# Attention scores and value products from high and low parts, one head at a time

## The chip, the core and the metric

The kernel runs on one core of a Trainium2 chip. The time is the device time of that core in microseconds (us). Three runs of the kernel before gave 1809.98, 1813.17 and 1820.33 us, so the median is 1813.17. The profile comes from a fourth execution of 1814.06 us, of which 1812.3 us lie between the first and the last instruction; the granted TensorE clock was 0.999 of full speed in it.

The engines are named as the profile names them: PE is TensorE (matrix products; PEld is its weight load), DVE is VectorE, ACT is ScalarE, POOL is GpSimd, SP is SyncE, which issues most DMAs.

## What is computed

Two layers over 256 latent tokens and 256 context tokens of width 2048. Layer 0 projects both streams, runs 16 heads of neighbourhood attention beside a bidirectional state-space mixer (SSD) of 8 groups, joins their outputs and projects them back. Layer 1 is a gated short convolution between two projections. Each layer's norm is modulated by a vector that is computed from a conditioning input with large weights. What matters here is the attention of one head (the reference, cut):

```
q = rms_norm(heads(p[Q]), q_norm_g);  k = rms_norm(heads(p[K]), k_norm_g);  v = heads(p[V])
s_lat = q @ k_window.T * scale + bias;   s_lat = where(mask, s_lat, -inf)
s_ctx = q @ k_ctx.T * scale
pr = softmax(concat([s_lat, s_ctx]))
out = pr @ concat([v_window, v_ctx]);   out = out * silu(gate_a)
```

Per head that is 256 queries against 512 keys (256 latent, with the window as an added mask, and 256 context) of 128 channels. All inputs are fp32.

## The kernel before

**Products in parts.** The large projections do not use full fp32 products. An operand is split into a high part, rounded to the type fp32r, and a low part, the rest: ACT casts (H = fp32r(w)), DVE subtracts (L = w - H). A product is then three fp32r products, H x H, H x L and L x H, that are summed in PSUM. For the weights this is done chunk by chunk: 1024 columns a chunk, cast by ACT at L409, subtracted by DVE at L416, into three buffers each (`wH`, `wL`). Small products, those of attention and of SSD among them, are done in full fp32 on the unsplit operands.

**Order of the work.** The kernel is written as one Python program that emits every engine's instructions in an order of its own. The main thread emits the projections for PE in a fixed order: in layer 0 the columns of K, V, Q and B of group 0 while the conditioning arrives, then for each of four head groups `a` (four heads each) Q, K, gate, V and the SSD columns, then the output projection `w_out`, then layer 1. Everything else is a task, a generator that yields what it waits for. Between the products, `pump` lets each task run on whose operands a table of costs and due times (`Plan`) counts as ready, so that attention, SSD and norms are woven into the stream of projections. Tasks have three classes: urgent, side (heads and SSD groups) and back. The one back task, `gemv_gen`, multiplies the conditioning weights on DVE (256 multiply-adds at L803, in 16 groups, each closed by four small matrix products into `mrow`) whenever DVE is ahead. The first four groups feed the end of layer 0, the twelfth (n = 11) is needed for the norm of layer 1 (`turn_gen` turns the new stream and scales it), the last before the output.

Each engine works its queue in the emitted order. PE's products wait for the splits of the weights; a wait at the head of ACT's or DVE's queue also holds back the weight splits behind it.

**One head.** `head_gen(a, h)` first loads the head's bias, adds the mask (L1003), and waits for `KT` and `QT`, the group's normed and transposed keys and queries. Then, for each half `qt` of the queries: one full fp32 product of 128 x 128 by 128 x 512 (`score`, L1008), bias and maximum on DVE (L1013), exp on ACT (L1018), scaling on DVE (L1023), four transposes on PE and a copy into `P` on ACT (L1050). `P` has two buffers, `PT0` and `PT1`, taken by even and odd heads. Last, four full fp32 products of 128 x 128 by 128 x 256 add up the values (L1058), DVE multiplies with the gate (L1062), and the head's output goes to the tensor `mixd` in DRAM. A head starts when the head two before it has done its value products. The output projection reads `mixd` back (L1491) and splits it (L1496 on ACT, L1497 on DVE).

Of the kernel before, what the change touches and what calls it, by code (L numbers as in the profile page):

```python
# [8 lines left out]
F32 = mybir.dt.float32  # L9
F32R = mybir.dt.float32r  # L10
AF = mybir.ActivationFunctionType
ALU = mybir.AluOpType
# [129 lines left out]
def kernel(ctx: ExitStack, tc, x, cx, ada_w, ada_b, w_in, w_out, sc_in, sc_out, rpb, small, const,  # L142
# [7 lines left out]
    V, S, G, T, DMA = nc.vector, nc.scalar, nc.gpsimd, nc.tensor, nc.sync  # L150
    DMA2 = nc.scalar
    plan = Plan()
    E = plan.add

    def st(shape, tag, dt=F32, name=None):
        return sb.tile(list(shape), dt, tag=tag, name=name or tag, bufs=1)
# [23 lines left out]
    KT, QT, Vt, gt = st([128, 4, 512], "KT"), st([128, 4, 256], "QT"), st([128, 4, 512], "Vt"), st([128, 4, 256], "gt")  # L180
    sz, xtm, yi = st([128, 4, 256], "sz"), st([128, 2, 512], "xtm"), st([128, 4, 256], "yi")
    PT = [st([128, 4, 256], f"PT{k}") for k in range(2)]
# [12 lines left out]
    four = lambda ap: ap.rearrange("p (a b) -> p a b", a=4)  # L195

    def mm(o, l, r, start, stop):
        E(T.matmul(o, l, r, start=start, stop=stop, skip_group_check=True))  # L198
# [7 lines left out]
    got = set()  # L206
# [128 lines left out]
    def bank():  # L335
        return take(free_b)

    def give(pool, *bs):
        pool.extend(bs)

    W_ = lambda eng, *aps, nb=0: (eng, aps, nb)
    when = lambda f: ("if", f, 0)
# [14 lines left out]
    RAW, HL = {}, {}  # L357
# [178 lines left out]
    for a in range(1, 4):  # L536
        qk = [(w_in, CQ(a), 512), (w_in, CK(a), 512)]
# [226 lines left out]
    bias = [st([128, 3, 256], f"bias{k}") for k in range(2)]  # L764
# [222 lines left out]
        got.add((key, a))  # L987

    b0 = rpbs[0, :, :]
    s4s = [st([128, 8], f"s4_{k}") for k in range(4)]  # L990

    def head_gen(a, h):
        hd = 4 * a + h
        bt, s4, P = bias[hd % 2], s4s[hd % 4], PT[hd % 2]
        yield when(lambda: hd < 2 or ("pv", hd - 2) in got)
        yield W_("SP")
        for r in range(4):
            E(DMA.dma_start(bt[64 * (r % 2):64 * (r % 2) + 64, r // 2, :].rearrange("p (a b) -> p a b", a=4),
                            bass.AP(tensor=b0.tensor, offset=b0.offset + hd * 64 * 320 + (7 - r) * 31 - 61,
                                    ap=[[319, 64], [31, 4], [1, 64]])))  # L1000
        yield W_("DVE", bt)
        bv = bt[:, 0:2, :].rearrange("p q (r c) -> p (q r) c", c=64)
        E(V.tensor_tensor(out=bv, in0=bv, in1=mask.unsqueeze(1).to_broadcast([128, 8, 64]), op=ALU.add))  # L1003
        sps = {}

        def score(qt):
            ps = bank()
            mm(ps, QT[:, h, qt * 128:(qt + 1) * 128], KT[:, h, :], True, True)  # L1008
            return ps

        def top(qt, ps):
            sp = sps[qt] = tmp()
            E(V.tensor_tensor_reduce(out=two(sp), in0=two(ps), in1=bt[:, 1:3, :] if qt else bt[:, 0::2, :], scale=1.0,  # L1013
                                     scalar=-3.0e38, op0=ALU.add, op1=ALU.max, accum_out=s4[:, qt:qt + 1]))
            give(free_b, ps)
            E(V.tensor_scalar(out=s4[:, 2 + qt:3 + qt], in0=s4[:, qt:qt + 1], scalar1=-1.0, scalar2=None, op0=ALU.mult))
            yield W_("ACT", sp, s4)
            E(S.activation(sp, sp, AF.Exp, bias=s4[:, 2 + qt:3 + qt], scale=1.0, accum_out=s4[:, 4 + qt:5 + qt]))  # L1018

        def scale_(qt):  # L1020
            sp = sps[qt]
            E(V.reciprocal(s4[:, 6 + qt:7 + qt], s4[:, 4 + qt:5 + qt]))
            E(V.tensor_scalar(out=sp, in0=sp, scalar1=s4[:, 6 + qt:7 + qt], scalar2=0.5, op0=ALU.mult, op1=ALU.mult))  # L1023

        def trans(qt):
            pt = bank()
            for kt in range(4):
                turn(pt[:, kt * 128:(kt + 1) * 128], sps[qt][:, kt * 128:(kt + 1) * 128])
            give(free_t, sps[qt])
            return pt  # L1030

        yield when(lambda: ("K", a) in got and ("Q", a) in got)
        yield ("grow", 2, 0)
        yield W_("PE", KT[:, h, :], QT[:, h, :], nb=1)
        p0 = score(0)
        yield W_("DVE", p0)
        yield from top(0, p0)
        yield W_("PE", nb=1)
        p1 = score(1)
        yield W_("DVE", p1)  # L1040
        yield from top(1, p1)
        yield W_("DVE", sps[0])
        scale_(0)
        yield W_("DVE", sps[1])
        scale_(1)
        for qt in range(2):
            yield W_("PE", sps[qt], nb=1)
            pt = trans(qt)
            yield W_("ACT", pt)
            E(S.copy(P[:, :, qt * 128:(qt + 1) * 128], four(pt)))  # L1050
            give(free_b, pt)
        yield ("cap", 0, 0)
        yield when(lambda: ("V", a) in got and ("G", a) in got)
        yield ("grow", 0, 1)
        yield W_("PE", P, Vt, nb=1)
        po = bank()
        for kt in range(4):
            mm(po[:, :256], Vt[:, kt, h * 128:(h + 1) * 128], P[:, kt, :], kt == 0, kt == 3)  # L1058
        got.add(("pv", hd))
        yield W_("DVE", po)  # L1060
        o = half()
        E(V.tensor_tensor(out=o, in0=po[:, :256], in1=gt[:, h, :], op=ALU.mult))  # L1062
        give(free_b, po)
        attn[0] += 2
        yield from put_mix(hd, o)
# [450 lines left out]
    def res_gen(k, c0, ps):  # L1516
# [29 lines left out]
    r1 = st([128, 2], "r1")  # L1546
    h1 = {}
    rb1 = []
    late = [PT[0][:, k, :] for k in range(4)] + [PT[1][:, k, :] for k in range(4)] + \
        [xtm[:, k // 2, (k % 2) * 256:(k % 2) * 256 + 256] for k in range(4)] + [yi[:, k, :] for k in range(4)]  # L1550

    held = {}

    def turn_gen():
        yield when(lambda: n_back[0] >= 11.5 and attn[0] == 32 and ssd_done[0] == 8)
        E(V.scalar_tensor_tensor(out=A1, in0=M1[:, 1], scalar=1.0, in1=P_("g1"), op0=ALU.add, op1=ALU.mult))
        for kp in range(0, KB, 2):
            yield when(lambda: ("x1", kp // 4) in got and (kp < 8 or len(passed) == 4))
            yield W_("PE", x1[0][:, kp * 128:(kp + 2) * 128], x1[1][:, kp * 128:(kp + 2) * 128], nb=1)
            pt = bank()  # L1560
            for b in range(2):
                for t in range(2):
                    turn(pt[:, b * 256 + t * 128:b * 256 + (t + 1) * 128], x1[t][:, (kp + b) * 128:(kp + b + 1) * 128])
            for b in range(2):
                kb = kp + b
                if kp < 8:
                    yield W_("ACT", pt)
                    E(S.activation(late[kb], pt[:, b * 256:(b + 1) * 256], AF.Copy, scale=A1[:, kb:kb + 1]))
                else:

                    held[kb] = pt
                got.add(("turn", kb))
            if kp < 8:
                give(free_b, pt)
        keep_up(8)
# [194 lines left out]
    for i in range(4):  # L1770
        for part, gen in ((1, cg_gen), (2, hv_gen), (0, bg_gen), (3, gg_gen)):
            ps = banks(4)
# [23 lines left out]
    for n in range(4):  # L1796
        if n == 1:
            force(lambda: n_back[0] >= 15, (urgent, back))
        ps = banks(2)
# [57 lines left out]
```

## Time and profile before

| | |
|---|---|
| median of 3 runs | 1813.17 us |
| the profiled execution | 1814.06 us |
| its span, first to last instruction | 1812.3 us |
| PE busy | 1775.1 us (98%) |
| DVE busy | 1259.2 us (69%) |
| ACT busy | 775.3 us (43%) |
| score products (L1008) | 32 in 64 records, 259.6 to 1181.5 us |
| value products (L1058) | 64 in 128 records, 277.0 to 1196.3 us |
| layer 1 begins | about 1360 us |

A full fp32 product shows as two matmul records, an fp32r product as one. Matmul records overlap, and the busy time of PE is time in which at least one is open, so what a product costs is read from the distance between starts or ends. Rows of the order of time begin with the start and the length in us; a bracket at the end gives the engine's idle time before the row and what ended it. Rows of groups give busy us, the mean length of one in ns, and the idle time before them. In rows of stretches the columns are named ahead of the rows.

### The profile page before, as it was taken

The page shows a single profiled execution, that of the slowest core. Times are in us where ns is not written, and L with a number is a line of the kernel's source. Part 1 is how long each engine was busy: PE and PEld are TensorE (multiplying, and loading weights), DVE is VectorE, ACT ScalarE, POOL GpSimd, SP SyncE. Part 2 cuts the span into 40 slices and gives each one's busy share as a digit, 9 for nine tenths or more (in the row PEclk, how much of TensorE's full clock was granted, in tenths as well). Part 3 has the DMA queues.
Part 4 walks back from the last instruction along what each step waited for, and adds up shares of the span by engine and source line. Part 5 has one row for each costly group of instructions (what it writes and reads, how often), then busy time and mean ns, then how long its engine had stood idle before and what let it go on. Part 6 is the DMA issues. An engine that isn't in the chain of part 4 may idle for free.

```text
span 1812.3 us, 26337 instructions
## 1 busy us (share of the span) xinstructions
PE 1775.1 (98%) x9961; PEld 1487.4 (82%) x9961; DVE 1259.2 (69%) x2041; ACT 775.3 (43%) x1362; POOL 30.5 (2%) x28
## 2 busy tenths in 40 slices
PE   5999999999999999999999999999999999999998
PEld 4677888888888888888888898778878888888887
DVE  5566875887575887575887687666667866665665
ACT  5422543455232455232454344544435444444442
POOL 0000100000000000000001000000000000000000
PEclk9999999999999999999999999999999999999999
DMA  9987654576655576655576566668776776666564
GB/s 337 342 289 254 196 163 135 169 217 202 204 168 168 170 220 198 218 165 169 170 221 186 165 185 185 205 211 300 268 248 203 241 231 188 190 192 188 192 211 153
DMA packets 249216, 376.90 MB, mean 208 GB/s; under 512 B 32656, under 2 KB 104048, under 8 KB 249088
## 3 DMA queue, kind: packets, MB, share of 16 engines
q1 hardware_dynamic: 239792, 366.64, 63.8%
q10 hardware_dynamic: 9296, 8.57, 1.4%
q8 instruction: 78, 1.28, 0.3%
q14 instruction: 50, 0.41, 0.1%
HBM read 368.70 MB, written 7.77 MB: 208 GB/s over the span
## 4 chain that ended last, share of the span: by engine, by line
PE 92%; DMA 3%; DVE 2%; issue 1%; ACT 1%; SPq 0%; POOL 0%; POOLq 0%; DVEq 0%; ACTq 0%
PE bank L198 90%; PE bank L202 3%; DMA raw<-in_ada_w 2%; DVE wL L416 1%; DVE acc L803 1%; DMA tmp<-dram_mixd 0%; DMA tmp<-dram_csr 0%; DVE hL L752 0%; SPq L566 0%; ACT wH L409 0%; DVE tmp L748 0%; ACT hH L746 0%; DVE xm L612 0%; ACT mix L1496 0%; DVE tmp L1790 0%
## 5 line engine op out<-in xcount | busy, mean ns | idle before, releaser
L409 ACT CAST wH<-raw 128x1024 fp32r<-128x1024 f32 (+1 forms) x440 | 459.0, 1044 | 701.2 <-PE bank L198 576.1
L416 DVE TENSOR_TENSOR wL<-raw,wH 128x1024 fp32r<-128x1024 f32 (+1 forms) x440 | 532.1, 1213 | 257.3 <-ACT wH L409 255.9
L198 PE MATMUL bank<-h,wH 128*128 128x512 f32 x1024 | 357.2, 395 | 2.7 <-ACT h L1636 1.5
L198 PE MATMUL bank<-hH,wH 128*128 128x256 f32 (+1 forms) x1040 | 352.6, 339 | 0.9 <-ACT wH L409 0.9
L198 PE MATMUL bank<-hL,wH 128*128 128x256 f32 (+1 forms) x1040 | 336.9, 324 | 0.0
L198 PE MATMUL bank<-hH,wL 128*128 128x256 f32 (+1 forms) x1024 | 331.2, 323 | 0.5 <-DVE wL L416 0.5
L198 PE MATMUL bank<-h,wL 128*128 128x256 f32 x1024 | 284.5, 278 | 0.0
L198 PE MATMUL bank<-wH,hH 128*128 128x512 f32 x640 | 257.4, 403 | 4.8 <-ACT hH L746 2.6
L198 PE MATMUL bank<-wL,hH 128*128 128x512 f32 x640 | 249.8, 391 | 0.3 <-DVE wL L416 0.3
L198 PE MATMUL bank<-wH,hL 128*128 128x512 f32 x640 | 249.3, 390 | 0.1
L803 DVE SCALAR_TENSOR_TENSOR acc<-raw,csil,acc 128x512 f32<-128x512 f32 x256 | 191.9, 750 | 65.5 <-DMA raw<-in_ada_w 52.0
L198 PEld LDWEIGHTS bank<-h,wH 128*128 128x128 f32 x1024 | 192.1, 188 | 49.1 <-issue 2.2
L198 PEld LDWEIGHTS bank<-hH,wH 128*128 128x128 f32 x1040 | 197.8, 190 | 23.2 <-issue 7.5
L198 PEld LDWEIGHTS bank<-hL,wH 128*128 128x128 f32 x1040 | 197.9, 190 | 19.8 <-issue 5.3
L198 PEld LDWEIGHTS bank<-hH,wL 128*128 128x128 f32 x1024 | 194.6, 190 | 16.5 <-DVE wL L416 1.1
L198 PEld LDWEIGHTS bank<-h,wL 128*128 128x128 f32 x1024 | 192.4, 188 | 0.0
L198 PE MATMUL bank<-wH,mix 128*128 128x512 f32 x512 | 164.1, 397 | 2.2 <-ACT wH L409 2.2
L198 PEld LDWEIGHTS bank<-wH,hH 128*128 128x128 f32 x640 | 120.2, 188 | 35.6 <-issue 7.5
L198 PEld LDWEIGHTS bank<-wH,hL 128*128 128x128 f32 x640 | 120.1, 188 | 25.4 <-DVE hL L752 0.6
L198 PEld LDWEIGHTS bank<-wL,hH 128*128 128x128 f32 x640 | 120.2, 188 | 24.3 <-DVE wL L416 1.1
L198 PEld LDWEIGHTS bank<-wH,mix 128*128 128x128 f32 x512 | 96.9, 189 | 23.4 <-ACT wH L409 2.7
L198 PE MATMUL bank<-wL,mix 128*128 128x512 f32 x256 | 100.6, 393 | 3.8 <-DVE wL L416 3.8
(244 smaller groups left out, 1662.9 us busy)
## 6 DMA issues: line engine op xcount, KB each, us to landing
raw<-in_w_in SPq DMA_DIRECT2D x209, 512.0 KB, 4.5
raw<-in_ada_w SPq DMA_DIRECT2D x163, 512.0 KB, 4.7
raw<-in_sc_in SPq DMA_DIRECT2D x128, 512.0 KB, 3.7
raw<-in_w_out SPq DMA_DIRECT2D x64, 512.0 KB, 4.3
raw<-in_sc_out SPq DMA_DIRECT2D x32, 512.0 KB, 4.5
tmp<-dram_csr SPq DMA_DIRECT2D x32, 256.0 KB, 7.1
PT<-in_ada_w SPq DMA_DIRECT2D x14, 512.0 KB, 5.8
yi<-in_ada_w SPq DMA_DIRECT2D x8, 512.0 KB
```

Source lines behind the costliest of these rows:

```text
L198: E(T.matmul(o, l, r, start=start, stop=stop, skip_group_check=True))
L202: E(T.transpose(o, i, ident if k == 128 else ident[:k, :k]))
L409: E(S.copy(H, v))
L416: E(V.tensor_tensor(out=Lo, in0=v, in1=H.bitcast(F32), op=ALU.subtract))
L803: E(V.scalar_tensor_tensor(out=acc, in0=v[:, j], scalar=csil[:, 2 * k + j:2 * k + j + 1], in1=acc, op0=ALU.mult, op1=ALU.add))
```

## The change

Keys, queries, softmax weights and values of a head are split into high and low parts, and each score and value product is made as three fp32r products. ACT casts `kH`, `qH`, `PH` (in place of the copy into `P`) and `vH`; DVE subtracts `kL`, `qL`, `PL` and `vL`. There is one buffer for each of these, `PH` and `PL` standing where `PT0` and `PT1` stood. So a head's keys are split only when the head before has emitted its second score, and its transposes wait until the head before has emitted its value products. In the norm of layer 1, the tiles that reused `PT0` and `PT1` are taken anew when `turn_gen` starts.

```diff
+    PH, PL = (st([128, 4, 256], f"PT{k}", F32R, name=f"P{'HL'[k]}") for k in range(2))
+    kH, kL, vH, vL = (st([128, 512], n, F32R) for n in ("kH", "kL", "vH", "vL"))
+    qH, qL = (st([128, 256], n, F32R) for n in ("qH", "qL"))
...
-        bt, s4, P = bias[hd % 2], s4s[hd % 4], PT[hd % 2]
+        bt, s4 = bias[hd % 2], s4s[hd % 4]
...
         def score(qt):
             ps = bank()
-            mm(ps, QT[:, h, qt * 128:(qt + 1) * 128], KT[:, h, :], True, True)
+            t = slice(qt * 128, (qt + 1) * 128)
+            mm(ps, qH[:, t], kH, True, False)
+            mm(ps, qL[:, t], kH, False, False)
+            mm(ps, qH[:, t], kL, False, True)
...
-        yield when(lambda: ("K", a) in got and ("Q", a) in got)
+        yield when(lambda: ("K", a) in got and ("Q", a) in got and (hd == 0 or ("qk", hd - 1) in got))
         yield ("grow", 2, 0)
-        yield W_("PE", KT[:, h, :], QT[:, h, :], nb=1)
+        yield W_("ACT", KT[:, h, :], QT[:, h, :])
+        E(S.copy(kH, KT[:, h, :]))
+        E(S.copy(qH, QT[:, h, :]))
+        yield W_("DVE", kH)
+        E(V.tensor_tensor(out=kL, in0=KT[:, h, :], in1=kH.bitcast(F32), op=ALU.subtract))
+        E(V.tensor_tensor(out=qL, in0=QT[:, h, :], in1=qH.bitcast(F32), op=ALU.subtract))
+        yield W_("PE", kL, qL, nb=1)
...
         p1 = score(1)
+        got.add(("qk", hd))
...
+        yield when(lambda: hd == 0 or ("pv", hd - 1) in got)
         for qt in range(2):
             yield W_("PE", sps[qt], nb=1)
             pt = trans(qt)
+            t = slice(qt * 128, (qt + 1) * 128)
             yield W_("ACT", pt)
-            E(S.copy(P[:, :, qt * 128:(qt + 1) * 128], four(pt)))
+            E(S.copy(PH[:, :, t], four(pt)))
+            yield W_("DVE", PH[:, :, t])
+            E(V.tensor_tensor(out=PL[:, :, t], in0=four(pt), in1=PH[:, :, t].bitcast(F32), op=ALU.subtract))
             give(free_b, pt)
...
-        yield W_("PE", P, Vt, nb=1)
+        yield W_("ACT", Vt)
+        vh = Vt[:, :, h * 128:(h + 1) * 128]
+        E(S.copy(four(vH), vh))
+        yield W_("DVE", vH)
+        E(V.tensor_tensor(out=four(vL), in0=vh, in1=four(vH).bitcast(F32), op=ALU.subtract))
+        yield W_("PE", PL, vL, nb=1)
         po = bank()
         for kt in range(4):
-            mm(po[:, :256], Vt[:, kt, h * 128:(h + 1) * 128], P[:, kt, :], kt == 0, kt == 3)
+            ks = slice(kt * 128, (kt + 1) * 128)
+            mm(po[:, :256], vH[:, ks], PH[:, kt, :], kt == 0, False)
+            mm(po[:, :256], vH[:, ks], PL[:, kt, :], False, False)
+            mm(po[:, :256], vL[:, ks], PH[:, kt, :], False, kt == 3)
...
-    late = [PT[0][:, k, :] for k in range(4)] + [PT[1][:, k, :] for k in range(4)] + \
+    late = [None] * 8 + \
...
     def turn_gen():
...
+        for k in range(2):
+            pl = st([128, 4, 256], f"PT{k}", name=f"late{k}")
+            late[4 * k:4 * k + 4] = [pl[:, q, :] for q in range(4)]
```

## The prediction, as it was made before the changed kernel was run

> **What bounds the kernel now.** I read the page first, then busy time by stretches, then the order of time around one head and around the place where attention hands over to the output projection.
>
> ```profile
> span 1812.3 us, 26337 instructions
> PE 92%; DMA 3%; DVE 2%; issue 1%; ACT 1%; SPq 0%; POOL 0%; POOLq 0%; DVEq 0%; ACTq 0%
> ...
> 260.00:1130.00 870.00, 870.00 (x4897) 737.80 (x4896) 636.81 (x1084) 356.68 (x693) 19.17 (x12) 1.00 0.61 184
> 1130.00:1220.00 90.00, 85.09 (x389) 67.71 (x388) 61.67 (x126) 46.06 (x92) 1.83 (x2) 0.98 0.64 208
> 1220.00:1340.00 120.00, 120.00 (x550) 98.75 (x549) 81.05 (x89) 52.08 (x63) 0.00 (x0) 1.00 0.81 274
> 1340.00:1375.00 35.00, 30.45 (x164) 25.04 (x163) 24.67 (x44) 15.98 (x26) 1.11 (x2) 1.00 0.58 200
> ```
>
> The columns of the stretches are length, then busy time of PE, PEld, DVE, ACT, POOL, the granted clock, DMA share and GB/s. From 260 to 1130 us PE has no gap, DVE is busy for 637 of 870 us, ACT for 357. The chain of waits is 92% PE. So a microsecond of PE work removed from that stretch is a microsecond of time, and DVE or ACT work added there costs nothing while DVE stays ahead of PE's needs. All of heads 0 to 11 lie in this stretch; heads 12 to 15 end in the next one, which has 4.9 us of PE gaps.
>
> **The change part by part.** *PE, scores.* One head's score is two matrix products of 128x512 in full fp32, each recorded as two passes; 16 heads make 32 products, 64 records.
>
> ```profile
> L198 PE MATMUL bank<-KT,QT 128*128 128x512 f32 x64 | 31.8, 594 | 0.0
> L198 PE MATMUL bank<-PT,Vt 128*128 128x256 f32 x128 | 29.8, 379 | 0.0
> ...
> 259.35 0.39 PE L198 MATMUL bank<-hL,wH 128*128 128x512 f32 x1
> 259.57 0.39 PE L198 MATMUL bank<-hH,wL 128*128 128x512 f32 x1
> 259.80 1.02 PE L198 MATMUL bank<-KT,QT 128*128 128x512 f32 x2
> 260.26 0.80 PE L198 MATMUL bank<-hH,wH 128*128 128x512 f32 x1
> 260.90 0.40 PE L198 MATMUL bank<-hL,wH 128*128 128x512 f32 x1
> ```
>
> Matmuls overlap, so the records' lengths are no prices; distances are. The hi/lo products of the projections, 128x512 with rounded fp32r operands, are the very kind that the change uses; a train of them gives their price, from its first to its last row 44 distances:
>
> ```profile
> 1116.35 0.39 PE L198 MATMUL bank<-wH,hH 128*128 128x512 f32 x1
> ...
> 1126.33 0.39 PE L198 MATMUL bank<-wH,hL 128*128 128x512 f32 x1
> ```
>
> (1126.33 - 1116.35) / 44 = 0.227 us. The score lies between the end of the matmul at 259.57 (259.57 + 0.39 = 259.96) and the end of the next projection product (260.26 + 0.80 = 261.06): 1.10 us, less that product's own 0.23, leaves 0.86 to 0.87. Three fp32r products cost 3 x 0.227 = 0.681. Gain 0.18 a score, 32 x 0.18 = 5.7 us.
>
> *PE, values.* One head has four 128x256 products, eight records.
>
> ```profile
> 306.10 0.39 PE L198 MATMUL bank<-hH,wL 128*128 128x512 f32 x1
> 306.33 1.89 PE L198 MATMUL bank<-PT,Vt 128*128 128x256 f32 x8
> 307.87 0.58 PE L198 MATMUL bank<-hH,wH 128*128 128x512 f32 x1
> ...
> 227.79 0.28 PE L198 MATMUL bank<-hH,wH 128*128 128x256 f32 x1
> 227.91 0.28 PE L198 MATMUL bank<-hL,wH 128*128 128x256 f32 x1
> 228.03 0.28 PE L198 MATMUL bank<-hH,wL 128*128 128x256 f32 x1
> ```
>
> The same reckoning: (307.87 + 0.58) - (306.10 + 0.39) - 0.23 = 1.73 us a head. A 128x256 fp32r product takes 227.91 - 227.79 = 0.12 us, each with its own weight load, so twelve take 1.44. Gain 0.29 a head, 16 x 0.29 = 4.6 us. PE in all: 5.7 + 4.6 = **10.3 us** less. The transposes stay as they are. Bounds: the widest distances in such trains are 0.24 (score: gain 0.14 x 32 = 4.5) and 0.125 (values: 0.23 x 16 = 3.7), so 8.2 at least; with the narrowest, 0.225 and 0.118, 11.1 at most.
>
> FP8 and Floating Point Precision (the Trainium skill, section TensorE Precision Notes) says that true FP32 takes four passes through the array. By that rule, with one pass priced like one fp32r product, the saving would be one product in four. The rows say 0.86 / 0.227 = 3.8 and 0.432 / 0.12 = 3.6 products, so they disagree by a little and I keep them; what four would give is a rival below.
>
> Where the scores now stand, PE's queue around the third score of before and the first one of the change (kH, kL are a head's keys, qH, qL its queries, hH and hL the projection's activations):
>
> ```order
> -L198 MATMUL bank_129<-KT,QT 128x512
>  L198 MATMUL bank_124<-hH_697,wH_136 128x512
>  L198 MATMUL bank_124<-hL_702,wH_136 128x512
>  L198 MATMUL bank_124<-hH_697,wL_139 128x512
> +L198 MATMUL bank_126<-kH,qH 128x512
> +L198 MATMUL bank_126<-kH,qL 128x512
> +L198 MATMUL bank_126<-kL,qH 128x512
> ```
>
> The first score moves some 5 us of projection products back, behind its subtractions; PE fills the time with projection work it has anyway, so the order of things changes but not their sum.
>
> *DVE and ACT.* Each head adds on DVE kL (128x512), qL (128x256), two PL (128x512 from PSUM) and vL (128x512), and on ACT kH, qH and vH; the two copies into P become casts. The nearest rows:
>
> ```profile
> L416 DVE TENSOR_TENSOR wL<-raw,wH 128x512 fp32r<-128x512 f32 x7 | 4.8, 688 | 0.7 <-ACT wH L409 0.7
> L1497 DVE TENSOR_TENSOR mix<-tmp,mix 128x256 fp32r<-128x256 f32 x32 | 12.0, 421 | 11.4 <-ACT mix L1496 11.4
> L945 DVE TENSOR_TENSOR tmp<-bank,statk 128x512 f32<-128x512 f32 x12 | 7.6, 682 | 0.0
> ...
> L409 ACT CAST wH<-raw 128x512 fp32r<-128x512 f32 x7 | 4.4, 623 | 17.8 <-PE bank L198 11.7 <-issue 5.4 <-ACT hH L746 0.7
> L1496 ACT CAST mix<-tmp 128x256 fp32r<-128x256 f32 x32 | 11.4, 403 | 9.1 <-DMA tmp<-dram_mixd 9.1
> L1050 ACT COPY PT<-bank 128x512 f32<-128x512 f32 x32 | 18.0, 589 | 36.0 <-PE bank L202 34.7 <-DMA dram_csr<-tmp 1.3
> ```
>
> DVE: 0.688 + 0.421 + 2 x 0.682 + 0.688 = 3.16 us a head, 50.6 us in all. ACT: 0.623 + 0.403 + 0.623 = 1.65, and 2 x (0.623 - 0.589) = 0.07 for the casts: 1.72 a head, 27 us in all. Cover: from 260 to 1130 DVE is idle for 233 us and ACT for 513; three quarters of the added work falls there (38 and 20 us). DVE's share rises from 73% to at most 78%. I take **0**. If the cover is gone, the whole 50.6 us lies bare; that end is the slower rival. Below nothing is excluded, since no wait of PE on DVE stands in that stretch to be shortened.
>
> What is queued behind the new subtractions on DVE is the next weight split, here wL_141, for which PE waits within two chunks. DVE's queue of the change at the first head:
>
> ```order
> L416 TENSOR_TENSOR wL_140<-raw_135,wH_137 128x1024
> L1200 SCALAR_TENSOR_TENSOR half_115<-bank_129,cwh,half_115 128x254
> L1006 TENSOR_TENSOR bias_213<-bias_213,const 128x512
> L1044 TENSOR_TENSOR kL<-KT,kH 128x512
> L1045 TENSOR_TENSOR qL<-QT,qH 128x256
> L416 TENSOR_TENSOR wL_141<-raw_131,wH_138 128x1024
> ```
>
> kL and qL, 1.11 us, stand ahead of wL_141. A chunk of 1024 weight columns feeds 24 products of 0.227, 5.5 us, when four row tiles use it, and 2.7 us in the output projection; a delay of 1.1 to 2.1 us (PL, PL, vL) fits in the first and just in the second.
>
> *One head at a time.* Single buffers for kH to vL and for PH and PL make head n+1 wait for head n's last value product before its transposes. Nobody but the next head group and the mix reads wait for that, and each has tens of microseconds of projection in between.
>
> *The filler work.* DVE also runs 256 multiply-adds of 0.75 us over the conditioning weights, in 16 groups, whenever it is ahead. 50.6 us more DVE work pushes four such groups (16 x 0.75 = 12 us each) out of attention into the stages behind. In PE's queue the matrix products that close a group stand with zero wait:
>
> ```profile
> L803 DVE SCALAR_TENSOR_TENSOR acc<-raw,csil,acc 128x512 f32<-128x512 f32 x256 | 191.9, 750 | 65.5 <-DMA raw<-in_ada_w 52.0 <-issue 5.7 <-DMA acc<-in_ada_b 2.9
> L198 PE MATMUL bank<-acc,const 128*32 128x128 f32 x128 | 6.8, 285 | 0.0
> ```
>
> The twelfth group must be through before layer 1's norm; its closing products now stand in the third pass of the output projection instead of before it, some 30 us of PE work ahead of need. I take 0.
>
> *The handover.* Here PE is not covered:
>
> ```profile
> 1154.55 0.39 PE L198 MATMUL bank<-wH,mix 128*128 128x512 f32 x1
> 1157.18 0.49 PE L198 MATMUL bank<-wH,mix 128*128 128x512 f32 x1 [2.23 <-ACT wH L409]
> 1159.41 0.56 PE L198 MATMUL bank<-wL,mix 128*128 128x512 f32 x1 [1.75 <-DVE wL L416]
> ...
> 1143.35 1.03 ACT L409 CAST wH<-raw 128x1024 fp32r<-128x1024 f32 x1
> 1153.85 0.71 ACT L1496 CAST mix<-tmp 128x256 fp32r<-128x256 f32 x2 [2.70 <-DMA tmp<-dram_mixd]
> 1155.47 0.71 ACT L1496 CAST mix<-tmp 128x256 fp32r<-128x256 f32 x2 [0.90 <-DMA tmp<-dram_mixd]
> 1156.08 1.04 ACT L409 CAST wH<-raw 128x1024 fp32r<-128x1024 f32 x1
> ...
> 1158.00:1164.00 6.00, 4.58 (x17) 3.40 (x18) 5.97 (x11) 5.72 (x13) 0.00 (x0) 0.72 0.59 175
> ```
>
> Between the weight casts of 1143.35 and 1156.08 ACT stands in line for reads of mixd; PE runs dry for 2.23 + 1.75 = 4.0 us, and right after it the granted clock is 0.72 for 6 us, another 6 x 0.28 = 1.7. ACT's queue there, before:
>
> ```order
> L1496 CAST mix_9075<-tmp_109 128x256
> L1491 DMA tmp_112<-dram_mixd 128x2x256
> L1348 ACTIVATE tmp_106<-tmp_106 128x256
> L1351 ACTIVATE tmp_106<-tmp_107,dtl 128x128 x2
> L1496 CAST mix_9084<-tmp_104 128x256
> L1496 CAST mix_9087<-tmp_104 128x256
> L1491 DMA tmp_109<-dram_mixd 128x2x256
> L1496 CAST mix_9091<-tmp_105 128x256
> L1496 CAST mix_9094<-tmp_105 128x256
> L1496 CAST mix_9100<-tmp_112 128x256
> L1496 CAST mix_9103<-tmp_112 128x256
> L409 CAST wH_136<-raw_133 128x1024
> ```
>
> and of the change:
>
> ```order
> L1521 CAST mix_9145<-tmp_105 128x256
> L1521 CAST mix_9148<-tmp_105 128x256
> L1516 DMA tmp_110<-dram_mixd 128x2x256
> L1373 ACTIVATE tmp_107<-tmp_107 128x256
> L1376 ACTIVATE tmp_107<-tmp_111,dtl 128x128 x2
> L1521 CAST mix_9183<-tmp_110 128x256
> L1521 CAST mix_9186<-tmp_110 128x256
> L1516 DMA tmp_108<-dram_mixd 128x2x256
> L1521 CAST mix_9190<-tmp_104 128x256
> L1521 CAST mix_9193<-tmp_104 128x256
> L1516 DMA tmp_113<-dram_mixd 128x2x256
> L409 CAST wH_138<-raw_132 128x1024
> ```
>
> The weight casts now stand a little closer together among the mix casts, but a later read of the last mixes has one weight cast less before it is waited for. I take 0 with both ends open: -5.7 if the dry spell goes, +5.7 if a second one like it comes.
>
> **Sum.** 1812.3 - 10.3 = 1802.0 us of span; the profiled execution took 1814.06, so 1803.8. The median of the runs, 1813.17, is 0.9 below that execution: **1803**. The forecast's own spread is 1800 to 1806.
>
> **The rivals.** (a) *The stall at the handover goes as well*: 1803 - 5.7 = 1797. For it: fewer mix casts between weight casts. Against: the same number of reads, as long to land. Chance 0.15. (b) *Four passes*: if a full fp32 product costs four fp32r products, the gain is 32 x 0.227 + 64 x 0.12 = 14.9 us and the time 1798. Against it the distances above, measured on these very instructions. 0.05. This is the page's rule cited above. (c) *Half the gain comes back as waits*: scores or values stand in PE's queue before kL or PL is ready, 0.32 us a head, or a second dry spell at the handover: 1803 + 5 = 1808. For it: DVE's in-order queue and the 4.0 us already lost there. Against: 870 us without one gap. 0.22. (d) *Slower*: DVE's subtractions delay the weight splits behind them and PE starves; the price is the bare part of 50.6 us. It eats the gain at 10.3 / 50.6 = 20% bare, and is slower by 0.5% (9.1 us) from 19.4 / 50.6 = 38%. Half bare: 1803 + 25 = 1828. Against: 233 us idle on DVE in that stretch. 0.07. The forecast keeps 0.51.
>
> **How the numbers follow.** Half a per cent, 9.1 us, is about what a measurement tells from no change; the border is 1804.1, only just above the forecast. Of the forecast's 0.51 I put 0.32 below the border and 0.19 above. Faster: 0.32 + 0.15 + 0.05 = 0.52. Same: 0.19 + 0.22 = 0.41. Slower: 0.07. The range 1796 to 1811 leaves out (d) and the outer parts of (a) and (c), about 0.17.
>
> **What would show it.** In the changed profile: kH, qH products 0.23 us apart and PH, vH products 0.12 apart; no idle time of PE put down to DVE kL, qL, PL or vL; DVE busy up by some 50 us and ACT by 27; PE still without gaps from 260 to 1120. I am wrong if PE shows idle time before those products, if the weight splits wL release PE often, or if the gaps of the handover change by more than 5 us.

## The result, and the profile after

Nine runs of the changed kernel gave a median of 1805.97 us (1800.62 to 1810.8), nine of the kernel before on the same chip 1815.35: ratio 0.9945, 95% interval [0.9928, 0.9963]. The same kernel was run once more later (twelve runs, median 1809.44; the kernel before 1814.86): 0.9965 [0.9952, 0.9978]. So the change makes the kernel faster by 0.35 to 0.55%, 5 to 9 us, on the border of what was taken as measurable. The profiled execution of the changed kernel, 1800.62 us, is the fastest of its nine; where it differs from the one of the repetition is told below.

The page after, its span, busy times and chain:

```profile
span 1798.8 us, 26647 instructions
PE 1765.1 (98%) x10057; PEld 1493.6 (83%) x10057; DVE 1302.0 (72%) x2121; ACT 796.7 (44%) x1410; POOL 31.1 (2%) x28
PE 91%; DMA 3%; DVE 3%; issue 1%; ACT 1%; SPq 0%; POOL 0%; POOLq 0%; DVEq 0%; ACTq 0%
```

PE's busy time fell by 10.0 us (from 1775.1), the span by 13.5. The same stretches as before, moved to where the stages now lie (columns: length, then PE, PEld, DVE, ACT, POOL, granted clock, DMA share, GB/s):

```profile
260.00:1122.00 862.00, 859.81 (x4943) 740.86 (x4942) 647.21 (x1106) 370.33 (x723) 20.15 (x12) 1.00 0.59 176
1122.00:1212.00 90.00, 89.14 (x450) 73.89 (x449) 72.96 (x145) 53.40 (x107) 1.43 (x2) 1.00 0.76 227
1212.00:1330.00 118.00, 118.00 (x540) 96.92 (x540) 76.39 (x86) 52.00 (x67) 0.00 (x0) 1.00 0.80 262
1330.00:1365.00 35.00, 31.59 (x178) 26.75 (x178) 26.75 (x52) 18.27 (x31) 1.11 (x2) 1.00 0.53 175
```

Attention shows 2.2 us of gaps where it had none, and the handover 0.9 us instead of 4.9. PE's order of time around the first score and the first value product:

```profile
263.49 0.40 PE L198 MATMUL bank<-hH,wL 128*128 128x512 f32 x1
263.72 0.39 PE L198 MATMUL bank<-kH,qH 128*128 128x512 f32 x1
263.95 0.40 PE L198 MATMUL bank<-kH,qL 128*128 128x512 f32 x1
264.19 0.39 PE L198 MATMUL bank<-kL,qH 128*128 128x512 f32 x1
264.42 0.39 PE L198 MATMUL bank<-hH,wH 128*128 128x512 f32 x1
...
283.83 0.28 PE L198 MATMUL bank<-PH,vH 128*128 128x256 f32 x1
283.95 0.28 PE L198 MATMUL bank<-PL,vH 128*128 128x256 f32 x1
...
285.12 0.28 PE L198 MATMUL bank<-PH,vL 128*128 128x256 f32 x1
```

A score takes 264.42 - 263.72 = 0.70 us (0.71 in the mean of all 32; it took 0.86). The twelve value products are (285.12 - 283.83) / 11 = 0.117 us apart, 1.41 us a head (1.73). By these rows PE saves 32 x 0.16 + 16 x 0.32 = 10.2 us. The new instructions of DVE and ACT, by groups (busy us, mean ns of one, idle time before them):

```profile
L1067 DVE TENSOR_TENSOR PL<-bank,PH 128x512 fp32r<-128x512 f32 x32 | 21.9, 686 | 6.1 <-ACT PH L1065 5.7
L1044 DVE TENSOR_TENSOR kL<-KT,kH 128x512 fp32r<-128x512 f32 x16 | 11.0, 686 | 3.5 <-ACT kH L1041 3.5
L1076 DVE TENSOR_TENSOR vL<-Vt,vH 128x512 fp32r<-128x512 f32 x16 | 10.9, 684 | 0.1
L1045 DVE TENSOR_TENSOR qL<-QT,qH 128x256 fp32r<-128x256 f32 x16 | 6.7, 420 | 0.0
...
L1065 ACT CAST PH<-bank 128x512 fp32r<-128x512 f32 x32 | 18.2, 586 | 30.5 <-PE bank L202 29.0 <-DVE half L1087 1.5
L1074 ACT CAST vH<-Vt 128x512 fp32r<-128x512 f32 x16 | 10.0, 624 | 0.6 <-DVE acc L793 0.6
L1041 ACT CAST kH<-KT 128x512 fp32r<-128x512 f32 x16 | 9.8, 614 | 1.3 <-PE bank L198 1.2
```

And from the list of what PE waited for in the whole run (us in all, times, longest; four longer rows, from the start and from the norm of layer 1, are left out):

```profile
PE bank L198 <- DVE wL L416: 1.4, 4, 0.5
PE bank L198 <- DVE tmp L1384: 1.2, 2, 1.0
...
PE bank L198 <- ACT Vt L972: 0.9, 1, 0.9
PE bank L198 <- ACT wH L409: 0.9, 1, 0.9
```

`kL`, `qL`, `PL` and `vL` are not in that list, and the 4.0 us for which PE ran dry at the handover before (2.23 on `wH`, 1.75 on `wL`) are gone; what PE waits there now is the 0.9 us on `Vt`.

To see where time went, I set the times of the projections' products, which every kernel here has in equal number (8224), side by side: time from one of them to the next mark, as a difference to the kernel before, in us.

| stretch, by number of the product | 900 to 4200: heads 0 to 11 | 4200 to 4950 | 4950 to 5100: heads 12 to 15, handover | 5100 to 5250 | 5250 to 5400: last reads of `mixd` | 5700 to 5850: norm of layer 1 | 6150 to 7800: layer 1 | all others | span |
|---|---|---|---|---|---|---|---|---|---|
| after | -8.8 | +1.3 | -10.0 | +2.9 | +0.5 | +0.6 | +3.5 | -3.5 | -13.5 |
| after, repeated | -8.4 | +1.3 | -5.0 | +2.9 | +0.6 | +0.6 | +3.5 | -2.5 | -7.0 |
| scores only | -5.3 | +3.7 | -9.5 | +1.7 | -0.2 | -1.5 | +3.3 | +0.5 | -7.3 |
| values only | -4.3 | -2.1 | -8.4 | +1.3 | +12.5 | -0.7 | +0.7 | -0.1 | -1.1 |
| values only, later use | -4.7 | -2.1 | -8.4 | +1.3 | +2.3 | -1.5 | +5.0 | -0.6 | -8.7 |
| subtractions twice | -3.6 | +1.3 | -8.4 | +0.7 | +19.2 | +28.6 | +3.6 | -2.2 | +39.2 |
| one product for three | -23.8 | -0.2 | -7.1 | -1.4 | +7.8 | +0.8 | +3.9 | -3.6 | -23.6 |

The columns don't hold the same work in every kernel: ahead of product 4200 the kernel before has 28 of the 32 scores (those of heads 12 and 13 too), the change 25, scores only 26.

### The profile page after: what moved, and what is told of

The parts are those of the page before. It is cut to its first block, busy times and chain, and to the rows that moved or that the text cites. A ratio compares the mean times of both kernels' runs of the same rounds, so it can differ in the third digit from the quotient of the medians.

```text
span 1798.8 us, 26647 instructions
## 1 busy us (share of the span) xinstructions
PE 1765.1 (98%) x10057; PEld 1493.6 (83%) x10057; DVE 1302.0 (72%) x2121; ACT 796.7 (44%) x1410; POOL 31.1 (2%) x28
## 4 chain that ended last, share of the span: by engine, by line
PE 91%; DMA 3%; DVE 3%; issue 1%; ACT 1%; SPq 0%; POOL 0%; POOLq 0%; DVEq 0%; ACTq 0%
PE bank L198 89%; PE bank L202 3%; DMA tmp<-dram_csr 2%; DVE wL L416 1%; DMA raw<-in_ada_w 0%; DMA tmp<-dram_mixd 0%; DVE acc L803 0%; DMA tmp<-in_x 0%; DVE hL L752 0%; SPq L566 0%; DVE tmp L1381 0%; DVE tmp L1200 0%; ACT wH L409 0%; DVE half L1396 0%; DVE tmp L748 0%
## 5 line engine op out<-in xcount | busy, mean ns | idle before, releaser
L198 PE MATMUL bank<-hH,wH 128*128 128x256 f32 (+1 forms) x1040 | 343.2, 330 | 0.9 <-ACT wH L409 0.9
L803 DVE SCALAR_TENSOR_TENSOR acc<-raw,csil,acc 128x512 f32<-128x512 f32 x256 | 191.8, 749 | 59.8 <-DMA raw<-in_ada_w 45.4
L198 PEld LDWEIGHTS bank<-hH,wH 128*128 128x128 f32 x1040 | 197.9, 190 | 18.7 <-issue 2.0
(259 smaller groups left out, 1790.1 us busy)
```

Source lines behind the costliest of these rows:

```text
L803: E(V.scalar_tensor_tensor(out=acc, in0=v[:, j], scalar=csil[:, 2 * k + j:2 * k + j + 1], in1=acc, op0=ALU.mult, op1=ALU.add))
```

## The experiments

My theory was that of the prediction: PE's products give the time, the splits are hidden. The rivals were that something of the gain comes back as waits, that holding a head to single buffers costs by itself, and that DVE's room is smaller than its idle time says.

**One half at a time.** The first kernel keeps `kH`, `kL`, `qH`, `qL` and their products and has the old value product on fp32 `P` and `Vt`; the second the other way round:

```diff
 scores only
-            mm(po[:, :256], vH[:, ks], PH[:, kt, :], kt == 0, False)   (and two more, with the splits)
+            mm(po[:, :256], Vt[:, kt, h * 128:(h + 1) * 128], P[:, kt, :], kt == 0, kt == 3)
 values only
-            mm(ps, qH[:, t], kH, True, False)                          (and two more, with the splits)
+            mm(ps, QT[:, h, qt * 128:(qt + 1) * 128], KT[:, h, :], True, True)
```

> Only the score products are made in three parts; the values stay full fp32 products with two P buffers. If PE's work alone sets the time, it falls by the score's share, 32 x (0.86 - 0.70) = 5 to 6 us, a ratio of 0.997 to the kernel before, and the handover's gaps stay as they fall. If the gain of the change came from its new order at the handover, the ratio is anything from 0.994 to 1.003 and follows the gaps between 1110 and 1220 us. If DVE's added work costs time, the ratio is 1.000 or above.

> Only the value products are made in three parts, with one buffer each for PH and PL; the scores stay full fp32 products. If PE's work alone sets the time, it falls by 16 x (1.73 - 1.40) = 5 us, a ratio of 0.997, and the two halves add up to the whole change. If the order at the handover decides, it follows the gaps there, 0.994 to 1.003. If DVE's work costs time, 1.000 or above, and more than for the scores, since two of the three subtractions of a head with PSUM operands are here.

Scores only: 1808.14 us, 0.9968 [0.9959, 0.9977]. That is some 6 us less, which agrees with PE's 5.1. In its profile heads 0 to 11 give 5.3, where PE alone would give 12 x 0.32 = 3.8 (two scores have moved out of that stretch), and other stretches gain and lose as much (-9.5, +3.7, +3.3 in the table), so the agreement is in part luck. Values only: 1813.02 us, 0.9991 [0.9981, 1.0002]. That is a miss. In attention its PE gain is there (-4.3 us in the table), but 12.5 us are lost in the output projection. Four instructions of that kernel in order of time, two of PE and two of ACT (ACTq issues DMAs), and the granted clock behind them:

```profile
1225.70 0.71 PE L198 MATMUL bank<-half,const 128*128 128x128 f32 x4
1242.38 0.79 PE L198 MATMUL bank<-wH,mix 128*128 128x512 f32 x1 [7.09 <-ACT mix L1510]
...
1235.41 0.38 ACTq L1505 DMA_DIRECT2D tmp<-dram_mixd  x1
1241.93 0.71 ACT L1510 CAST mix<-tmp 128x256 fp32r<-128x256 f32 x2 [5.55 <-DMA raw<-in_w_out]
...
1238.30:1248.50 10.20, 6.12 (x14) 4.78 (x15) 2.27 (x4) 1.31 (x3) 0.00 (x0) 0.50 0.72 264
```

The product of `half` and `const` closes the norm of the last SSD group. Its output goes to `mixd`, is read back at 1235.41, cast at 1241.93, and PE, which has come to the product that needs it, has stood for 7.1 us. The clock is at half for 10.2 us, from within the wait on; PE works for 6.1 of them, so that costs 3.1 more: 10.2 of the 12.5. The idle time of ACT is put down to a weight load by the profile; the cast is that of `tmp`, which the read of 1235.41 fills. The row holds two casts of 0.40 us; the product starts right after the first of them (1241.93 + 0.40 = 1242.33). In the changed kernel the same steps:

```profile
1211.37 0.61 PE L198 MATMUL bank<-half,const 128*128 128x128 f32 x4
1231.25 0.62 PE L198 MATMUL bank<-wH,mix 128*128 128x512 f32 x2
...
1217.51 0.41 ACTq L921 DMA_DIRECT2D dram_mixd<-half  x1
1223.64 0.37 ACTq L1516 DMA_DIRECT2D tmp<-dram_mixd  x1
1229.91 0.71 ACT L1521 CAST mix<-tmp 128x256 fp32r<-128x256 f32 x2
```

From the product to the end of the first cast 1229.91 + 0.40 - 1211.37 = 18.9 us pass, and the product that waited in the other kernel is the second of the row at 1231.25, begun at 1231.48. The changed kernel makes this deadline by 1.2 us; in the repetition's profile, too, by 1.2. In the kernel before:

```profile
1196.56 0.61 PE L198 MATMUL bank<-half,const 128*128 128x128 f32 x4
1246.21 0.62 PE L198 MATMUL bank<-wH,mix 128*128 128x512 f32 x2
...
1213.72 0.71 ACT L1496 CAST mix<-tmp 128x256 fp32r<-128x256 f32 x2 [1.47 <-DMA tmp<-dram_mixd]
```

There the casts were through by 1213.72 + 0.71 = 1214.43, and the product (the second of the row at 1246.21) used them at 1246.43, 32 us later.

**The gates alone.** Full fp32 products and no splits, but one buffer `P`, and each head held back until the one before has emitted its scores and its value products:

```diff
-        bt, s4 = bias[hd % 2], s4s[hd % 4]
+        bt, s4, P = bias[hd % 2], s4s[hd % 4], PT[0]
```

> The kernel before with full fp32 products, one P buffer and the two new conditions (one head at a time), and nothing else. If heads one at a time cost nothing, the ratio is 0.998 to 1.002. If the waits cost something that the change earns back, it is 1.002 to 1.005, with PE gaps between 260 and 1130 us.

1815.23 us, 1.0007 [0.9998, 1.0015]: one head at a time costs nothing in sum. But that is two things that cancel: heads 0 to 11 lose 4.8, where PE stands for 2.7 us on a `tmp` of SSD and half clock costs another 1.7, and the handover gains 7.4, where 0.9 us of gaps are left of 4.0.

**PE's share.** All splits are made, but only the product of the high parts is computed:

```diff
-            mm(ps, qH[:, t], kH, True, False)
-            mm(ps, qL[:, t], kH, False, False)
-            mm(ps, qH[:, t], kL, False, True)
+            mm(ps, qH[:, t], kH, True, True)
```

and alike for the values.

> All casts and subtractions of the change stay, but each score and value product is the high parts' product alone (the low parts' products are left out). PE then has 32 x 2 x 0.227 + 64 x 2 x 0.12 = 29.9 us less than the changed kernel. If PE sets the time throughout attention, it falls by 28 to 31 us against the changed kernel, a ratio of 0.978 to the kernel before. If DVE's or ACT's added work is close to setting the time, less than 20 us come, a ratio above 0.984, and PE shows idle time put down to kL, PL, vL or wL.

1790.1 us, 0.9856 [0.9841, 0.987]. Taken out are 64 x 0.233 + 128 x 0.117 = 29.9 us of PE; the median is 16 us below the first set of the change and 19 below the repetition, not the 28 to 31 that I had named for a kernel that PE bounds throughout. Three quarters of the 29.9 us, 22.4, belong to heads 0 to 11, whose stretch gives 15 us more than the change. Of this kernel's list of waits of PE the two largest after the start are:

```profile
PE bank L198 <- DVE tmp L1380: 6.8, 5, 2.8
PE bank L198 <- ACT mix L1517: 4.8, 1, 4.8
```

One is SSD's work, and 4.5 of its 6.8 us lie in the stretch of heads 0 to 11, where PE stands for 7.4 us in all and runs 3.4 us at half clock. The other is the same last read of `mixd`. The waits on `PL` and `wL` that I had named as a sign are small (0.8 and 0.4 us in that stretch). So PE is the bound only until the next deadline, and a further saving on PE loses part of itself there.

**DVE's room.** Each new subtraction is made twice, with the same operands (50.6 us more on DVE):

```diff
+        E(V.tensor_tensor(out=kL, in0=KT[:, h, :], in1=kH.bitcast(F32), op=ALU.subtract))
+        E(V.tensor_tensor(out=qL, in0=QT[:, h, :], in1=qH.bitcast(F32), op=ALU.subtract))
...
+            E(V.tensor_tensor(out=PL[:, :, t], in0=four(pt), in1=PH[:, :, t].bitcast(F32), op=ALU.subtract))
...
+        E(V.tensor_tensor(out=four(vL), in0=vh, in1=four(vH).bitcast(F32), op=ALU.subtract))
```

> The changed kernel with each of the five subtractions of a head made twice: 16 x 3.16 = 50.6 us more on DVE, nothing else. If DVE's idle time covers it, the ratio to the kernel before stays at that of the change, 0.992 to 0.997. If the cover is used up, PE idles on wL, kL or PL and the time rises by up to 50 us, a ratio of up to 1.022; half bare is 1.008.

1853.28 us, 1.021 [1.0189, 1.0231]: 2.1% slower than before, 47 us more than the first set of the change and 44 more than the repetition. But attention hardly pays, and of the waits that I had named only 3.8 us on `wL` show: heads 0 to 11 lose 5 us against the change, the last reads of `mixd` 18.7, the norm of layer 1 28. PE's long waits in this kernel and the clock at the norm:

```profile
PE bank L198 <- DVE acc L803: 18.6, 1, 18.6
...
PE bank L198 <- ACT mix L1525: 8.6, 1, 8.6
PE bank L202 <- DMA rowb<-dram_mrow: 4.6, 1, 4.6
PE bank L198 <- DVE half L1636: 4.0, 1, 4.0
...
1362.00:1393.00 31.00, 6.50 (x34) 5.61 (x35) 8.23 (x15) 2.38 (x6) 0.90 (x1) 0.50 0.30 92
```

The wait on `acc` is the filler: the multiply-adds at L803 up to 1340 us, in the kernel before, the changed one and this one (length, DVE busy and count, clock, DMA share, GB/s):

```profile
0.00:1340.00 1340.00, 173.93 (x232) 1.00 0.67 210
...
0.00:1340.00 1340.00, 145.35 (x194) 1.00 0.67 206
...
0.00:1340.00 1340.00, 133.25 (x178) 0.99 0.65 199
```

Twelve groups, which layer 1's norm needs, are 192. The change stands at 194, this kernel at 178, and PE waits.

**Where in attention the DVE work is added.** The same doubling for heads 0 to 3, for heads 12 to 15, and for heads 0 to 7 (`if hd < 4:`, `if hd >= 12:`, `if hd < 8:` ahead of each doubled line).

> The changed kernel with the subtractions made twice in heads 0 to 3 alone, 12.6 us more on DVE early in attention. If DVE's idle time in attention covers subtractions, the ratio to the kernel before stays that of the change, 0.993 to 0.998. If subtractions lie bare wherever they are, the time rises by 10 us or more against the change, a ratio above 1.000.

> The same 12.6 us, in heads 12 to 15 alone. If the weak place is the tail of attention, where the last heads' outputs must reach the output projection in time, the time rises by 8 to 20 us against the change (as in the stretch around the 5300th projection product when all heads were doubled), a ratio of 1.000 to 1.007, with PE gaps put down to ACT mix. If DVE's load as such decides, this run and the one with heads 0 to 3 take the same time.

> The subtractions made twice in heads 0 to 7, 25.3 us more on DVE. The filler's twelfth group then closes so late that the transposition of its result stands right at the norm of layer 1. If the filler's lateness is what made the run with all heads doubled slow, PE idles there for 4 to 10 us on the read of that result and the ratio is 0.998 to 1.004. If attention itself pays, the loss lies between 260 and 1100 us instead.

1821.17 us, 1.0035 [1.0019, 1.0051]; 1824.66, 1.0047 [1.003, 1.0064]; 1825.35, 1.0051 [1.0036, 1.0067]. They hold 12.6, 12.6 and 25.3 us of DVE work and cost 12 to 15, 15 to 19 and 16 to 19 us, against the repetition and the first set of the change: in four heads about as much as the work itself or more, in eight heads less. By stretches against the first profile of the change, heads 0 to 3 cost +6.4 in attention and +10.6 at the last reads of `mixd`; heads 12 to 15 cost +20.5 at those reads alone; heads 0 to 7 cost +4.9, +15.7, and +1.9 at the norm, where I had looked for 4 to 10. The last is a miss, in the ratio too. Heads 0 to 3 fit neither of the two cases that I had named: they are not covered, but attention itself pays only 6.4 us for them. The wait of the second, and its clock:

```profile
1248.35 0.79 PE L198 MATMUL bank<-wH,mix 128*128 128x512 f32 x1 [9.15 <-ACT mix L1529]
...
1236.80:1253.90 17.10, 7.37 (x25) 5.53 (x26) 4.98 (x12) 1.42 (x4) 0.20 (x1) 0.50 0.64 213
```

So the place of the added work decides little: early or late, half of the loss or more is paid at the same product, which waits for the last SSD group's output.

**What the reads of `mixd` hang on.** The planner, which decides what is emitted when, takes a read on ACT's queue as landed 1500 ns after its data could have come. With 5000 the casts of mix go later in ACT's queue. The same edit in the changed kernel and in the kernel before:

```diff
-                done = free = max(self.dma, s + 1000) + n / self.RATE + 1500
+                done = free = max(self.dma, s + 1000) + n / self.RATE + 5000
```

> The changed kernel with one number of the planner changed: DMAs that ACT issues are counted as landing 3.5 us later, so that casts of mixd reads are emitted later and weight casts before them. If PE's dry spells at the handover cost the change something, the time falls by up to 2 us against the changed kernel; if they are gone already, it stays within 2 us.

> The kernel before with the same number changed. If the dry spell at the handover (4.0 us of gaps and 1.7 us at a low granted clock) is in its usual time, the time falls by 4 to 6 us, a ratio of 0.997, and the gaps of 2.23 and 1.75 us are gone from the profile. If the spell was only in the one profiled execution, the ratio is 0.999 to 1.001.

In the changed kernel 1818.15 us, 1.0015 [1.0001, 1.0029], in the kernel before 1812.62, 0.9982 [0.997, 0.9994]. In the kernel before, PE's waits on the weight cast and split are gone from the handover, but two others stand there:

```profile
PE bank L198 <- DVE tmp L1359: 1.8, 1, 1.8
PE bank L198 <- ACT Vt L972: 1.7, 1, 1.7
```

They are 3.5 us where there were 4.0, but the clock stays at 1.00. The median is 2.2 us below that of the kernel before in the same set (3.3 by the ratio), less than the 4 to 6 that I had looked for. So what the old dry spell costs in the usual run is not settled. For the changed kernel I had expected 2 us at most either way, and it is 8.7 us above the repetition: the number pushed the last SSD group's norm later, PE waited 7.4 us on the same mix cast, and half clock went with it.

The cause of the last loss can now be set out over all kernels. For each I counted, in the order in which PE's instructions are emitted, how much projection work (by the distances of its products) lies between the closing product of the last SSD group and the first product that needs its result:

| kernel | work between, us | wait of PE on the mix cast, us |
|---|---|---|
| scores only | 59 | 0 |
| before, with 5000 | 49 | 0 |
| before | 48 | 0 |
| gates only | 22 | 1.4 |
| values only, later use (below) | 20 | 0.2, on the low part |
| after, and repeated | 19 | 0 |
| subtractions twice, heads 0 to 3 | 14 | 7.7 |
| one product for three | 11 | 4.8 |
| values only | 9 | 7.1 |
| after, with 5000 | 9 | 7.4 |
| subtractions twice, heads 0 to 7 | 5 | 11.3 |
| subtractions twice, heads 12 to 15 and all | 0 | 9.2 and 8.6 |

With 48 us or more no kernel waits, with 14 or less all do; the change stands between, at 19, where the gates alone (22) already wait for 1.4, since the way itself is not equally long everywhere (24.5 us there, 18.9 in the change). The row of the gates alone, which adds nothing to DVE, shows as well what took most of the room: of the 29 us that the change lost, 26 go with holding each head until the one before is through its value products. Scores only, which keeps two buffers `P` and so lacks that gate, has 59. The doublings show that DVE's work takes the rest when there is more of it. Each of these is one order that the planner found: its number 5000 alone, with the same gates, takes the change from 19 to 9.

**Later use.** If that is the cause, values only must get its gain back when the last group's output is merely used later. I took the kernel with values only and put the blocks of the output projection in another order:

```diff
-    order = list(range(0, 6)) + list(range(8, 16)) + [6, 7]
+    order = list(range(0, 6)) + list(range(8, 14)) + [6, 14, 7, 15]
```

> The kernel with the values alone in three parts, and one list changed: the output projection takes the last two SSD blocks and the last heads in the order 6, 14, 7, 15 instead of 14, 15, 6, 7, so that the last SSD group's output is used 11 us of PE work later. If the late reading of that output is what ate the values' gain, PE's wait of 7.1 us on ACT mix and the 10 us at half clock behind it go, 10 to 12 us come back and the ratio falls from 0.9991 to 0.992 to 0.995. If the values' split costs its time elsewhere, the ratio stays above 0.997.

1806.1 us, 0.995 [0.9935, 0.9966], against 0.9991 without the reordering. That is 7 us where I had expected 10 to 12: the table of stretches has +2.3 where there was +12.5, but layer 1 takes 4.3 more (+5.0 and +0.7). The same steps in this kernel:

```profile
1223.91 0.71 PE L198 MATMUL bank<-half,const 128*128 128x128 f32 x4
...
1243.31 0.71 ACT L1510 CAST mix<-tmp 128x256 fp32r<-128x256 f32 x2 [0.56 <-DMA tmp<-dram_mixd]
1245.06 0.73 PE L198 MATMUL bank<-wH,mix 128*128 128x512 f32 x2 [0.23 <-DVE mix L1511]
```

The cast comes no earlier than in values only (1241.93 there), PE now needs it later and waits 0.2 us. So it is the use of that output so soon that cost values only its gain. The ratio is no price of the values' products, though: 0.5% is more than PE's 5.1 us, and this kernel is also without the old dry spell (-8.4 us at the handover, as in values only).

**The change once more**, with no edit, for the spread between runs:

> The changed kernel once more, on the chip of this set. The ratio should be 0.993 to 0.997. If the dry spell at the handover is a matter of luck in how reads land, its profile may show it again (up to 4 us of PE gaps between 1130 and 1170 us); if the new order removed it, the gaps there stay under 1 us as in the first profile of the change.

1809.44 us, 0.9965 [0.9952, 0.9978]. Its profile (span 1805.3 us) differs from the first one by 5.0 us at the handover and otherwise by less than 1.2 in any stretch. There PE stood twice, and lost clock (a stretch of 8 us):

```profile
1148.38 0.43 PE L198 MATMUL bank<-tmp,xtm 128*64 128x128 f32 x2 [1.96 <-ACT Vt L972]
1149.63 1.11 PE L198 MATMUL bank<-tmp,xtm 128*64 128x128 f32 x6 [0.81 <-DVE tmp L1384]
...
1148.00:1156.00 8.00, 6.80 (x23) 5.29 (x24) 6.30 (x15) 5.09 (x11) 0.00 (x0) 0.57 0.78 242
```

Two gaps of together 2.8 us, and half clock for 8 x 0.43 / 0.5 = 6.8 us, of which PE works 6.0: 3.0 more. Less the 0.9 us gap that the first profile has there, that is 4.9 of the 5.0 us. So one and the same kernel has this dry spell in one execution and not in another; that it makes the spread of the other runs too (10.2 us in the first set) is likely, but only the two profiles show it.

## Why the prediction was right, point by point

- **The sum.** 1803 us with 1796 to 1811; measured 1806 and 1809. By ratio, 0.9944 forecast, 0.9945 and 0.9965 measured.
- **PE, scores and values.** 5.7 + 4.6 = 10.3 us forecast; 5.1 + 5.1 = 10.2 by the profile. A score's products are 0.23 apart as expected, but three of them, to the start of the next product, take 0.70 and not 0.681; the value products are a little closer than 0.12. In attention up to head 11, where PE alone should give 12 x 0.64 = 7.7 us, the two profiles show 8.8 and 8.4, scores alone 5.3, values alone 4.3 to 4.7. That is less close than it looks: three scores (3 x 0.86 = 2.6 us) and the closing products of two filler groups (0.7) have left that stretch, and PE stands there for 2.2 and 2.4 us. One sign that was named failed: PE was to stay without gaps up to 1120 us, and stands for 2.2.
- **Four passes** (the rival from the Trainium skill, FP8 and Floating Point Precision, section TensorE Precision Notes): PE's busy time fell by 10.0 us and not by 14.9. The rows decide: a full fp32 product here is worth 3.8 or 3.6 fp32r products.
- **DVE and ACT at nothing.** The durations held: 686, 420, 686, 684 ns and 614, 586, 624. The records add up to 50.5 us on DVE; the page's busy time rose by 42.8, since neighbouring records overlap; ACT's busy time rose by 21.4, where 27 were forecast, while the lengths of its records add up to 27.1 more. No product waits for `kL`, `qL`, `PL` or `vL`. From 260 to 1130 us DVE takes on 38 us of subtractions and drops 28 multiply-adds of the filler (178 to 150, 21 us).
- **The cover was named wrongly.** I measured it by DVE's idle time in attention, 233 us. Twice the subtractions showed that attention pays 5 us for 38, while the limits lie behind it: the last read of `mixd` has 1.2 us left, the twelfth filler group 2 multiply-adds by 1340 us. The slower rival (d) had its price in the wrong place: not weight splits, but these two deadlines, and it is nearer than 0.07 suggests (12.6 us more, in four heads, make the kernel 0.35 and 0.47% slower than before).
- **"Each has tens of microseconds of projection in between"** is the step that failed. For heads it is true of the next head group. For the mix reads the last SSD group, not a head, is the last to come, and its norm product moved from 48 us ahead of its use to 19, nearly all of it (to 22) in the kernel with the gates alone; the way through `mixd` takes 18.9. I priced a wait there at nothing without looking up the distance; that it was nothing was luck: 1.2 us were left.
- **The filler.** Four groups pushed back were forecast; 38 multiply-adds, 2.4 groups, are (232 to 194 at 1340 us). The closing product of the twelfth still has no wait: right, but with less room than the "some 30 us" of PE work, since what counts is when DVE is through.
- **The handover.** I took 0 with -5.7 and +5.7 as ends. From product 4200 to 5250 the change is -5.8 us in the first profile and -0.8 in the repetition. The heads there give nothing in sum: values 4 x 0.32 = 1.3 less, but seven scores lie there instead of four, 7 x 0.70 - 4 x 0.86 = 1.5 more. The old dry spell, 5.7, is gone in both, and so is a gap of 0.9 ahead of 1216.02; 0.9 comes in its place in the first and 5.8 in the second (2.8 + 3.0). That makes -5.5 and -0.6, all but 0.3 and 0.2 of what was measured; a few transposes and closing products that change places are left out. Rival (a) was half true: that dry spell goes, but another comes in some executions.
- **What was not foreseen and isn't settled.** Layer 1 (products 6150 to 7800) takes 3.5 us longer, without gaps, in both profiles of the change and +3.8 with the gates alone, which splits nothing. Filler moved there explains about 1.1 us in the change (the closing products of three more groups). The other 2.4 are no gap: the 1649 products of the stretch stand further apart, on average 234.1 ns behind a product with `wH` and 117.0 behind one with `wL`, against 232.7 and 115.4 in the kernel before (236.0 and 116.8 with the gates alone). Why stays open.

So PE's 10.2 us are right, but the number came out through other terms as well: heads 0 to 11, the handover and layer 1 make -8.8 - 5.8 + 3.5 of the first profile's -13.5 us and -8.4 - 0.8 + 3.5 of the repetition's -7.0. That what I had at nothing nearly cancelled is luck.

## What to carry to other kernels

A gain at the bound engine holds as far as the next deadline behind it. When work is added on a covered engine, don't ask how idle that engine is, but which result that it delays has the least slack: count, in the bound engine's own order, the work between the product that makes a result and the one that uses it, and set that against the time of the way between (write, read, cast). Here one buffer less, with the gates that it needs, took a result from 48 us ahead of its use to 22 at no cost in sum; the change stood at 19, and 12.6 us more of hidden work cost it 12 to 19.

## What the hardware showed that was not expected

- Idle time of PE was often paid twice. With a gap of 7.1 us went 10.2 us at a granted clock of 0.50, with one of 9.2 (after two of 1.9 and 1.7) 17.1, with the waits at the norm about 31. The length of these stretches was 3.4, 6.8, 10.2, 17.1 us: about multiples of 3.4. The kernel before ran 3.4 us at half clock after gaps of 2.23 and 1.75 us, and the repetition 6.8 after 1.96 and 0.81. The Trainium skill (TensorE: Matmul & The Clock Gate, section HAM oscillation — how this bites in real kernels) warns of idle gaps above about 3.4 us; here two shorter ones within 3 to 5 us were enough. With the gates alone a single gap of 1.6 us, ended at 678.37, was followed by half clock for 3.4 us from 679.68; but in the kernel before with 5000 the gaps of 1.8 and 1.7 us, 6 us apart, left the clock at 1.00. What decides is not shown.
- The way of one SSD group's output to its use (PE's last product, two steps of DVE, write to DRAM, read, cast) took 16.2 to 19.4 us to the start of the cast (values only, the change, values only with later use). In values only the read alone took 6.5 of them (1235.41 to 1241.93), although each of its two tiles is only 128x256. ACT's queue adds to it: in values only the read of 1235.41 was issued behind weight casts that go at PE's pace of 2.7 us each.
